# Third and fourth column groups of the modulation: steps of four contraction tiles instead of two

## The chip, the cores and the metric

The kernel runs on one core of a Trainium2 chip. The metric is the device time of one execution in microseconds (us). The time before is 2145.62 us, the median of three runs that lay between 2143.08 and 2147.35 us. A profile is one further execution with its own time.

The engines are named as in the profile: PE is the matrix engine (PEld its loading of the stationary operand), DVE the vector engine, ACT the scalar engine, POOL the general one, and SP issues almost all DMA transfers, in one queue that it works through in order.

## The reference, cut to what matters

One encoder layer on x of 1024 x 2048, all in 32-bit floats. What the change touches is the first line of it, the modulation of the normalized input by the condition c:

```python
mod = silu(c) @ w_ada + b_ada            # c: 2048, w_ada: 2048 x 6144
shift, scale, gate = split(mod, 3)
h = rmsnorm(x, pre_g) * (1 + scale) + shift
proj = h @ w_in                          # 2048 x 4608, and h @ w_merge, 2048 x 4096
...
```

The rest (windowed attention, multi-scale pooling, two gated branches, the output projection and a second norm) follows and is not touched.

## The kernel before, in words

**Products.** A big product is made in blocks of 256 output columns. Each block is one call of `strassen` and takes seven smaller products in place of eight. The banks that they sum into are called X, V and Z, so on PE one reads the sequence X, V, Z, X, V, Z and a last Z, which comes two products later, behind the first two of the next block (`run` calls `flush` there). A 32-bit operand is split into two parts (names ending in `h`/`l`, and `whi`/`wlo` for weights), and each product has the three part products high-high, low-high and high-low. ACT makes the high part (line 95), DVE the low one (line 96).

**The ramp.** At the start not all of h is there. So the first four blocks (`RAMP = 4`) are made in two halves: first over contraction groups j = 0 and 1 (`ramp_gen(0, i)`), where a product is six matmuls on PE, and later over j = 2 and 3 (`ramp_gen(1, i)`), with the first half's results loaded back and added. `fill(j)` multiplies two row tiles of x by the scale and adds the shift, and makes from them the seven split moving operands (B11, T3, T2, B21, T4, T1, B22) of group j. It needs `modc[..., j]`, which is what the change is about.

**The modulation.** `modulation(j, ...)` makes shift and scale of column group j: silu(c) times 16 contraction tiles of w_ada, each 128 x 512. The stationary operand `scz[:, kc, :]` has 32 columns, of which one is used, so a matmul takes a quarter of the array's columns; tile `kc` goes to quarter `kc % 4` and to 32 of the 128 partitions of a bank named GEMV (line 453). Each 32-bit matmul stands in the profile as two, so 16 tiles are 32 rows there. After the last tile ACT copies the bank (`acc`), PE adds up the four quarters (bank PM, line 424), and DVE adds the bias (`modc`, line 428). Groups 0 and 1 run before the ramp. The third and fourth (j = 2 and 3) are cut into eight steps of two tiles each, put into a queue `side`, 16 steps long. Three of them run before the ramp; then `run` takes one out after each step of the ramp's blocks (I call these places slots, numbered from 0). With `pin` the tile framework keeps these matmuls in the place where the code has them; other instructions are ordered by the framework's own scheduler.

**Where the tiles come from.** The 16 tiles of group j = 2 are loaded by `ada_slots(2)`, each in a buffer of its own (line 438). Those of j = 3 lie in five buffers of two tiles each, loaded ahead (`ada_tile`, line 417); buffers six to eight reuse the first three, so that their loads wait until PE has read the old tiles. In SP's queue these late loads stand behind the stores of the first ramp block's results (`ramp_d`, line 311).

Of the kernel before, what the change touches and what calls it, by code (L numbers as in the profile page):

```python
# [42 lines left out]
def encoder_layer(ctx: ExitStack, tc: tile.TileContext, x, c, table, w_ada, b_ada, pre_g,  # L43
# [32 lines left out]
    def uid(s):  # L76
        cnt[0] += 1
        return f"{s}_{cnt[0]}"

    def bank(tag, name="b"):  # L80
        return psum.tile([P, 512], F32, tag=tag, name=uid(name), bufs=1 if tag in SEEDED else 2)
# [268 lines left out]
    for r0, src in ((0, c[0]), (16, b_ada[0, 0:D]), (32, b_ada[0, D:2 * D]),  # L350
                    (48, pre_g[0]), (64, b_merge[0]), (96, pool_scale[0])):
        n = src.shape[0] // P
# [68 lines left out]
    def sum_columns(acc):  # L421
        pm = bank("at", "PM")
        for g in range(4):
            nc.tensor.matmul(pm[:, g:g + 1], acc[:, g, :], ones, start=True, stop=True)
        return pm

    def mod_columns(j, pm):
        tc.keep_in_program_order(nc.vector.tensor_tensor(
            modc[:, :, :, j], pm[:, 0:4].rearrange("p (g h) -> p g h", g=2),
            cols[:, 16:48].rearrange("p (g k) -> p g k", g=2)[:, :, 2 * j:2 * j + 2], ALU.add))  # L430
        nc.vector.scalar_tensor_tensor(modc[:, 1, :, j], modc[:, 1, :, j], 1.0,
                                       cols[:, 48 + 2 * j:50 + 2 * j], op0=ALU.add, op1=ALU.mult)

    def ada_slots(j):
        tiles = []
        for kc in range(KT):
            tiles.append(slot("ada", F32, (P, 4, P)))
            load(tiles[kc].rearrange("p (g h) n -> p g (h n)", g=2),
                 w_ada[kc * P:(kc + 1) * P, 0:2 * D].rearrange("p (g n) -> p g n", g=2)
                 [:, :, j * 256:(j + 1) * 256])  # L440
        return tiles

    def modulation(j, tile_of, pin=False):

        st_ = {}

        def step(q):
            if q == 0:
                st_["pv"] = bank("at", "GEMV")
            pv = st_["pv"]  # L450
            for kc in (2 * q, 2 * q + 1):
                g = kc % 4 * 32
                ins = nc.tensor.matmul(pv[g:g + 32, :], scz[:, kc, :], tile_of(kc), start=kc < 4,  # L453
                                       stop=kc >= 12, tile_position=(0, g))
                if pin:
                    tc.keep_in_program_order(ins)
            if q == 7:
                acc = xa2.tile([P, 4, P], F32, tag="acc", name=uid("acc"), bufs=2)
                tc.keep_in_program_order(
                    nc.scalar.activation(acc, pv.rearrange("p (g n) -> p g n", g=4), AF.Copy))  # L460
                mod_columns(j, sum_columns(acc))

        return [lambda q=q: step(q) for q in range(8)]

    def weigh(acc, t, kc):

# [7 lines left out]
    def modulation_steps(j):  # L474

        st_ = {}

        def step(q):
            if q == 0:
                st_["acc"] = xa2.tile([P, 4, P], F32, tag="acc", name=uid("acc"), bufs=2)  # L480
            if q == 8:
                mod_columns(j, st_["pm"])
                return
            acc = st_["acc"]
            at = ada_tile(j, q)
            for kk in range(2):
                kc = q * 2 + kk
                weigh(acc, at[:, kk], kc)
            if q == 7:
                st_["pm"] = sum_columns(acc)  # L490

        return [lambda q=q: step(q) for q in range(9)]
# [46 lines left out]
    ada = [ada_slots(0), ada_slots(1)]  # L539
# [8 lines left out]
            ada3.append(ada_tile(3, kc // 2))  # L548
        return ada3[kc // 2][:, kc % 2]

    side = deque(modulation(2, ada[2].__getitem__, True) + modulation(3, tile3, True))
    for s in range(2):
        for si in range(4 * s, 4 * s + 4):
            norm_rows(si)
# [16 lines left out]
        nc.tensor.matmul(bank(tag, "OPEN"), hi[:, 0:P], hi, start=True, stop=True)  # L571


    for _ in range(3):
        side.popleft()()
    parts = {}
    for i in range(RAMP):
# [126 lines left out]
    side = deque(s_ for j in range(4, 8) for s_ in modulation_steps(j))  # L704
# [47 lines left out]
    def x_step(n):  # L752
        if n < 2 * NB:
            held[n] = fetch_x(n // 2, n % 2)
        if n >= 2:
            turn_x((n - 2) // 2, n % 2, held.pop(n - 2))

    side = deque(lambda n=n: x_step(n) for n in range(2 * NB + 2))
# [17 lines left out]
    side = deque()  # L776
# [12 lines left out]
    with pool("attn") as ap:  # L789
        kv = {}  # L790

        def take_kv(kvh, what):
            hi = ap.tile([P, S], F32R, tag=what + "hi", name=uid(what))
            lo = ap.tile([P, S], F32R, tag=what + "lo", name=uid(what))
            col = (COL_K if what == "k" else COL_V) + kvh * P
            for s in range(2):
                sl = slice(s * 512, (s + 1) * 512)
                raw = ap.tile([P, 512], F32, tag="raw", name=uid("kvr"), bufs=2)
                load(raw, proj_d[col:col + P, sl])
                src = raw  # L800
                if what == "v":
                    src = bank("at")
                    for j in range(4):
                        nc.tensor.transpose(src[:, j * P:(j + 1) * P], raw[:, j * P:(j + 1) * P], ident)
                split(hi[:, sl], lo[:, sl], src)
            kv[what] = (hi, lo)


        qraw, q, bt, g, pr, pv = {}, {}, {}, {}, {}, {}
# [3 lines left out]
        def fetch_q(u):  # L813
            hp, j = UNITS[u]
            for e in range(2):
                h = 2 * hp + e
                if j == 0:
                    bt[e] = ap.tile([P, SPAN], F32, tag=f"bt{e}", name=f"bt{h}")
                    load(bt[e], bass.AP(bias_d.tensor, bias_d[h].offset + 127, [[LINE - 1, P], [1, SPAN]]))
                qraw[e] = ap.tile([P, 512], F32, tag="raw", name=uid("qr"), bufs=2)  # L820
                load(qraw[e], proj_d[COL_Q + h * P:COL_Q + (h + 1) * P, j * P:j * P + 512])

        def split_q(e):
            hi = ap.tile([P, 512], F32R, tag=f"qhi{e}", name=uid("qhi"))
            lo = ap.tile([P, 512], F32R, tag=f"qlo{e}", name=uid("qlo"))
            nc.scalar.activation(hi, qraw[e], AF.Copy, scale=P ** -0.5)
            nc.vector.scalar_tensor_tensor(lo, qraw[e], P ** -0.5, f32(hi), op0=ALU.mult, op1=ALU.subtract)
            q[e] = hi, lo
# [36 lines left out]
        def turn(u, e):  # L865
            _, n = blk(UNITS[u][1])
            if e == 0:
                pv[u] = [ap.tile([P, 3, 2, P], F32R, tag=f"pp{i}", name=uid("pp")) for i in range(2)]
            p = pr.pop((u, e))
            pt = bank("at", "PT")  # L870
            for i in range(n):
                nc.tensor.transpose(pt[:, i * P:(i + 1) * P], p[:, i * P:(i + 1) * P], ident)
            split(pv[u][0][:, 0:n, e], pv[u][1][:, 0:n, e], pt[:, 0:n * P].rearrange("p (b q) -> p b q", b=n))

        def values(u):
            hp, j = UNITS[u]
            b0, n = blk(j)
            (vhi, vlo), (phi, plo) = kv["v"], pv.pop(u)
            po = bank("at", "PV")[:, 0:2 * P]
            for i in range(n):  # L880
                ks = slice((b0 + i) * P, (b0 + i + 1) * P)
                nc.tensor.matmul(po, vhi[:, ks], phi[:, i], start=i == 0, stop=False)
                nc.tensor.matmul(po, vhi[:, ks], plo[:, i], start=False, stop=False)
                nc.tensor.matmul(po, vlo[:, ks], phi[:, i], start=False, stop=i == n - 1)
            qs = slice(j % 4 * P, (j % 4 + 1) * P)
            for e in range(2):
                nc.vector.tensor_tensor(g[e][:, qs], po[:, e * P:(e + 1) * P], g[e][:, qs], ALU.mult)
                if j % 4 == 3:
                    h = 2 * hp + e
                    store(ya_d[h * P:(h + 1) * P, (j - 3) * P:(j + 1) * P], g[e])  # L890

        def step(u, e):
            nu = len(UNITS)
            if e == 0 and 0 <= u - LAG_V < nu:
                values(u - LAG_V)
            if 0 <= u - LAG_T < nu:
                turn(u - LAG_T, e)
            if u < nu:
                if u % 16 == 0 and e == 0:
                    take_kv(UNITS[u][0] * 2 // GQA, "k")  # L900
                if u % 4 == 0:
                    split_q(e)
                scores(u, e)
            if e == 1:
                if u % 4 == 3 and u + 1 < nu:
                    fetch_q(u + 1)
                c_ = u - LAG_V + 1
                if 0 <= c_ < nu:
                    if c_ % 16 == 0:
                        take_kv(UNITS[c_][0] * 2 // GQA, "v")  # L910
                    if c_ % 4 == 0:
                        open_gate(c_)
# [372 lines left out]
    side = deque()  # L1285
# [123 lines left out]
```

## Time and profile before

| what | value |
|---|---|
| median of the runs | 2145.62 us (2143.08 to 2147.35) |
| the profiled execution, its own time | 2142.59 us |
| its span, first to last instruction | 2140.8 us |
| PE busy | 2096.1 us, 98% of the span |
| DVE busy | 1537.3 us, 72% |
| ACT busy | 1129.5 us, 53% |
| mean granted clock of PE | 0.997 |
| DMA moved | 466.11 MB, 218 GB/s in the mean |

The profiled execution lies 3.0 us below the median of the runs, and its time is 1.8 us above its span. A row of a timeline gives start, duration, engine, line, operation, what it writes and reads, shapes and a count; behind it, in brackets, the engine's idle time just before and what ended it. Matmuls overlap, and their ends are modelled, so distances are best read from start to start.

### The profile page before, as it was taken

The page shows a single profiled execution, that of the slowest core. Times are in us where ns is not written, and L with a number is a line of the kernel's source. Part 1 is how long each engine was busy: PE and PEld are TensorE (multiplying, and loading weights), DVE is VectorE, ACT ScalarE, POOL GpSimd, SP SyncE. Part 2 cuts the span into 40 slices and gives each one's busy share as a digit, 9 for nine tenths or more (in the row PEclk, how much of TensorE's full clock was granted, in tenths as well). Part 3 has the DMA queues.
Part 4 walks back from the last instruction along what each step waited for, and adds up shares of the span by engine and source line. Part 5 has one row for each costly group of instructions (what it writes and reads, how often), then busy time and mean ns, then how long its engine had stood idle before and what let it go on. Part 6 is the DMA issues. An engine that isn't in the chain of part 4 may idle for free.

```text
span 2140.8 us, 28950 instructions
## 1 busy us (share of the span) xinstructions
PE 2096.1 (98%) x9567; PEld 1715.2 (80%) x9567; DVE 1537.3 (72%) x2754; ACT 1129.5 (53%) x2124; POOL 7.4 (0%) x66
## 2 busy tenths in 40 slices
PE   6999999999999999999999999999999999999998
PEld 4588888887878888888888888888788888778886
DVE  5786666777547676777776788666956977879667
ACT  5654444443474546767775433333645644667654
POOL 0000000000000000000000000000000000000000
PEclk9999999999999999999999999999999999999999
DMA  9986566898766356445454766765655655696996
GB/s 331 292 277 202 188 207 202 305 315 270 237 216 213 122 169 207 157 156 197 150 165 154 235 214 203 242 193 171 228 170 166 213 192 164 219 298 219 303 306 240
DMA packets 303255, 466.11 MB, mean 218 GB/s; under 512 B 23882, under 2 KB 144866, under 8 KB 303104
## 3 DMA queue, kind: packets, MB, share of 16 engines
q1 hardware_dynamic: 301648, 462.02, 65.6%
q0 software_dynamic: 1120, 2.19, 0.3%
q8 instruction: 75, 1.23, 0.2%
q14 instruction: 76, 0.62, 0.1%
q10 hardware_dynamic: 336, 0.06, 0.0%
HBM read 340.41 MB, written 125.85 MB: 218 GB/s over the span
## 4 chain that ended last, share of the span: by engine, by line
PE 80%; DMA 8%; DVE 7%; issue 2%; ACT 2%; SPq 0%; ACTq 0%; DVEq 0%
PE Z L235 26%; PE V L235 18%; PE X L235 17%; PE Z L1139 2%; PE Z L1141 2%; PE Z L1140 2%; DVE wlo L96 2%; DMA raw<-in_w_merge_dram 1%; PE V L1141 1%; PE V L1139 1%; PE V L1140 1%; PE X L1141 1%; PE X L1140 1%; PE X L1139 1%; PE GEMV L453 1%
## 5 line engine op out<-in xcount | busy, mean ns | idle before, releaser
L95 ACT ACTIVATE whi<-raw 128x512 fp32r<-128x512 f32 (+1 forms) x528 | 319.7, 609 | 504.5 <-PE Z L235 252.6
L96 DVE TENSOR_TENSOR wlo<-raw,whi 128x512 fp32r<-128x512 f32 (+1 forms) x528 | 346.6, 662 | 189.8 <-PE Z L235 116.5
L96 DVE TENSOR_TENSOR wlo<-wr,whi 128x512 fp32r<-128x512 f32 x224 | 151.1, 689 | 60.9 <-ACT whi L95 58.5
L95 ACT ACTIVATE whi<-wr 128x512 fp32r<-128x512 f32 x224 | 138.5, 629 | 92.8 <-DVE wlo L96 35.9
L102 DVE TENSOR_TENSOR raw<-raw,raw 128x512 f32<-128x512 f32 x80 | 55.2, 690 | 94.2 <-DMA raw<-in_w_merge_dram 70.8
L1078 ACT ACTIVATE gt<-gt,cols 128x512 f32<-128x512 f32 x64 | 46.1, 722 | 96.2 <-DMA gt<-proj_d 77.8
L235 PE MATMUL V<-T3h,whi 128*128 128x512 f32 x336 | 92.9, 396 | 3.3 <-DVE u L102 3.3
L235 PE MATMUL X<-B11h,whi 128*128 128x512 f32 x336 | 92.4, 393 | 1.7 <-DVE part L102 0.9
L235 PE MATMUL Z<-B22h,whi 128*128 128x512 f32 x336 | 92.4, 395 | 0.8 <-ACT u L290 0.8
L235 PE MATMUL V<-T4h,whi 128*128 128x512 f32 x336 | 92.0, 393 | 0.4 <-ACT T4h L95 0.4
L235 PE MATMUL Z<-T1h,whi 128*128 128x512 f32 x336 | 91.8, 392 | 0.3 <-ACT T1h L95 0.3
L235 PE MATMUL V<-T3l,whi 128*128 128x512 f32 x336 | 91.5, 392 | 0.0
L235 PE MATMUL Z<-T1l,whi 128*128 128x512 f32 x336 | 91.1, 390 | 0.2
L235 PE MATMUL X<-B11l,whi 128*128 128x512 f32 x336 | 91.1, 390 | 0.2 <-DVE B11l L96 0.2
L235 PE MATMUL Z<-T2h,whi 128*128 128x512 f32 x336 | 91.2, 392 | 0.0
L235 PE MATMUL V<-T4l,whi 128*128 128x512 f32 x336 | 91.0, 390 | 0.0
L235 PE MATMUL X<-B21h,whi 128*128 128x512 f32 x336 | 90.9, 391 | 0.0
L235 PE MATMUL V<-T4h,wlo 128*128 128x512 f32 x336 | 90.8, 390 | 0.0
L235 PE MATMUL Z<-B22l,whi 128*128 128x512 f32 x336 | 90.8, 390 | 0.0
L235 PE MATMUL Z<-T1h,wlo 128*128 128x512 f32 x336 | 90.8, 390 | 0.0
L235 PE MATMUL Z<-T2l,whi 128*128 128x512 f32 x336 | 90.7, 390 | 0.0
L235 PE MATMUL V<-T3h,wlo 128*128 128x512 f32 x336 | 90.6, 390 | 0.0
(306 smaller groups left out, 4847.0 us busy)
## 6 DMA issues: line engine op xcount, KB each, us to landing
part<-part_d SPq DMA_DIRECT2D x136, 256.0 KB, 4.8
ada<-in_w_ada_dram SPq DMA_DIRECT2D x128, 256.0 KB, 4.7
raw<-in_w_in_dram SPq DMA_DIRECT2D x64, 512.0 KB, 4.1
raw<-in_w_merge_dram SPq DMA_DIRECT2D x64, 512.0 KB, 5.7
wr<-ws_dS SPq DMA_DIRECT2D x64, 512.0 KB, 5.3
wr<-in_w_out_dram SPq DMA_DIRECT2D x48, 512.0 KB, 5.0
proj_d<-part SPq DMA_DIRECT2D x68, 256.0 KB, 2.2
sw<-in_w_out_dram SPq DMA_DIRECT2D x64, 256.0 KB, 5.4
```

Of the source, the lines that this page charges most:

```text
L95: ins = (nc.scalar.activation(hi, src, AF.Copy), nc.vector.tensor_tensor(lo, src, f32(hi), ALU.subtract))
L96: nc.vector.tensor_tensor(lo, src, f32(hi), ALU.subtract))
L102: return (eng or nc.vector).tensor_tensor(o, a, b, ALU.add)
L235: nc.tensor.matmul(ps, w_[:, i], op[mov][j][m_], start=fresh and i == 0 and n == 0, stop=i == nj - 1 and n == 2, skip_group_check=True)
L453: ins = nc.tensor.matmul(pv[g:g + 32, :], scz[:, kc, :], tile_of(kc), start=kc < 4, stop=kc >= 12, tile_position=(0, g))
L1078: nc.scalar.activation(gt, gt, AF.Sigmoid, bias=cols[:, col:col + 1])
L1139: nc.tensor.matmul(pb, hi, w[0], start=first, stop=False, skip_group_check=True)
L1140: nc.tensor.matmul(pb, lo, w[0], start=False, stop=False, skip_group_check=True)
L1141: nc.tensor.matmul(pb, hi, w[1], start=False, stop=last, skip_group_check=True)
```

## The change

A step now sums four tiles, one for each quarter of the array's columns, and a group has four steps instead of eight. The fourth group's steps no longer follow one another from slot to slot: the queue is padded with empty steps, so that they stand at its places 6, 9, 12 and 15. Two steps instead of three run before the ramp, so in slots the third group's last steps stand at 0 and 1 (before: 0 to 4), and the fourth group's at 4, 7, 10 and 13 (before: 5 to 12).

```diff
-            for kc in (2 * q, 2 * q + 1):
+            for kc in range(4 * q, 4 * q + 4):
                 g = kc % 4 * 32
                 ins = nc.tensor.matmul(pv[g:g + 32, :], scz[:, kc, :], tile_of(kc), start=kc < 4,
                                        stop=kc >= 12, tile_position=(0, g))
                 if pin:
                     tc.keep_in_program_order(ins)
-            if q == 7:
+            if q == 3:
                 acc = xa2.tile([P, 4, P], F32, tag="acc", name=uid("acc"), bufs=2)
...
-        return [lambda q=q: step(q) for q in range(8)]
+        return [lambda q=q: step(q) for q in range(4)]
...
-    side = deque(modulation(2, ada[2].__getitem__, True) + modulation(3, tile3, True))
+    side = deque(modulation(2, ada[2].__getitem__, True))
+    for n, step in zip((6, 9, 12, 15), modulation(3, tile3, True)):
+        side.extend([lambda: None] * (n - len(side)) + [step])
...
-    for _ in range(3):
+    for _ in range(2):
         side.popleft()()
```

All that the change moves lies in the first ramp half. Behind the first product of the third ramp block, PE's instructions stand in the same order in both programs. Two places show what moved.

The first is PE at the fourth group's first step. Before, this step (tiles `ada_388`, both halves of one buffer) stands after the fifth product of the first ramp block (bank V, operand T4):

```order
L235 MATMUL V_740<-T4h_367,wlo_798 128x512
L453 MATMUL GEMV_809<-ada_388,scz 32x512 x2
L235 MATMUL Z_739<-T1h_311,whi_812 128x512
L235 MATMUL Z_739<-T1h_371,whi_812 128x512
L235 MATMUL Z_739<-T1l_312,whi_812 128x512
L235 MATMUL Z_739<-T1l_372,whi_812 128x512
L235 MATMUL Z_739<-T1h_311,wlo_813 128x512
L235 MATMUL Z_739<-T1h_371,wlo_813 128x512
L453 MATMUL GEMV_809<-ada_391,scz 32x512 x2
```

Now it stands one product earlier, after the fourth (bank X, operand B21), and takes the tiles of two buffers:

```order
L235 MATMUL X_740<-B21h_363,wlo_784 128x512
L453 MATMUL GEMV_797<-ada_388,scz 32x512 x2
L453 MATMUL GEMV_797<-ada_391,scz 32x512 x2
L235 MATMUL V_742<-T4h_307,whi_802 128x512
L235 MATMUL V_742<-T4h_367,whi_802 128x512
L235 MATMUL V_742<-T4l_308,whi_802 128x512
```

So tile 3 of the group (second half of `ada_391`) is wanted two products earlier than before, and three full products now follow without a step between.

The second place is PE at the third step of the fourth group. Before, tiles 8 and 9 (`ada_400`) and 10 and 11 (`ada_889`, the sixth buffer) had a product between them:

```order
L453 MATMUL GEMV_809<-ada_400,scz 32x512 x2
L235 MATMUL Z_829<-T2h_299,whi_877 128x512
L235 MATMUL Z_829<-T2h_359,whi_877 128x512
L235 MATMUL Z_829<-T2l_300,whi_877 128x512
L235 MATMUL Z_829<-T2l_360,whi_877 128x512
L235 MATMUL Z_829<-T2h_299,wlo_878 128x512
L235 MATMUL Z_829<-T2h_359,wlo_878 128x512
L453 MATMUL GEMV_809<-ada_889,scz 32x512 x2
```

Now the four stand together after that product:

```order
L235 MATMUL Z_829<-T2h_359,wlo_876 128x512
L453 MATMUL GEMV_797<-ada_400,scz 32x512 x2
L453 MATMUL GEMV_797<-ada_889,scz 32x512 x2
L235 MATMUL X_828<-B21h_303,whi_894 128x512
```

The loads of the sixth to eighth buffers keep their places in SP's queue: behind the stores of the first ramp block, and the eighth buffer's second half behind that block's last store.

## The prediction

> **What bounds the kernel now.** I read the page's head first, then busy time by stretch, then PE's timeline through the ramp, then SP's queue and its landings.
>
> ```profile
> span 2140.8 us, 28950 instructions
> PE 2096.1 (98%) x9567; PEld 1715.2 (80%) x9567; DVE 1537.3 (72%) x2754; ACT 1129.5 (53%) x2124; POOL 7.4 (0%) x66
> ```
> ```profile
> 60.00:78.00 18.00, 17.10 (x73) 8.19 (x74) 14.15 (x30) 11.69 (x23) 0.00 (x0) 1.00 1.08 348
> 78.00:96.00 18.00, 18.00 (x77) 9.38 (x76) 11.68 (x25) 10.15 (x21) 0.00 (x0) 1.00 0.74 233
> 96.00:114.00 18.00, 18.00 (x81) 14.90 (x80) 17.23 (x38) 15.28 (x34) 0.00 (x0) 1.00 0.85 268
> ```
> (Columns: stretch, length, busy time of PE, PEld, DVE, ACT, POOL, granted clock, DMA share, GB/s.) PE sets the time nearly everywhere, so PE time taken out of a stretch without PE idling shortens the run. But up to 78 us the DMA engines are full (348 GB/s), and what PE does there waits for tiles. After 78 us DMA has room, while weight loads of PE (9.38 of 18) show that PE's time goes elsewhere: into the steps.
>
> PE's timeline:
>
> ```profile
> 57.52 2.42 PE L453 MATMUL GEMV<-ada,scz 128*32 128x512 f32 x12
> ...
> 65.63 1.07 PE L453 MATMUL GEMV<-ada,scz 128*32 128x512 f32 x8
> 66.63 0.73 PE L235 MATMUL Z<-T2l,whi 128*128 128x512 f32 x2
> 67.20 0.62 PE L235 MATMUL Z<-T2h,wlo 128*128 128x512 f32 x2
> 67.75 1.05 PE L453 MATMUL GEMV<-ada,scz 128*32 128x512 f32 x4
> 68.73 0.73 PE L235 MATMUL X<-B21h,whi 128*128 128x512 f32 x2
> ...
> 73.78 1.05 PE L453 MATMUL GEMV<-ada,scz 128*32 128x512 f32 x4
> ...
> 74.76 0.74 PE L235 MATMUL Z<-T1h,whi 128*128 128x512 f32 x2
> ...
> 77.35 0.73 PE L235 MATMUL X<-B11h,whi 128*128 128x512 f32 x2
> ...
> 79.92 0.74 PE L235 MATMUL V<-T3h,whi 128*128 128x512 f32 x2
> ...
> 82.51 0.73 PE L235 MATMUL Z<-B22h,whi 128*128 128x512 f32 x2
> ...
> 92.83 0.73 PE L235 MATMUL Z<-T1h,whi 128*128 128x512 f32 x2
> ...
> 93.86 0.95 PE L424 MATMUL PM<-ones,acc 128*128 128x1 f32 x8
> ...
> 95.21 0.63 PE L235 MATMUL X<-B11h,whi 128*128 128x512 f32 x2
> ...
> 96.60 0.62 PE L235 MATMUL V<-T3h,whi 128*128 128x512 f32 x2
> ...
> 104.77 0.62 PE L235 MATMUL X<-B11h,whi 128*128 128x512 f32 x2
> ...
> 106.13 0.62 PE L235 MATMUL V<-T3h,whi 128*128 128x512 f32 x2
> ```
>
> Three prices follow. A product without a step: 106.13 - 104.77 = 1.36 us. A product with a step of two tiles: 79.92 - 77.35 = 2.57, so the step costs 1.21. And a step of four tiles is in this trace already: at 65.63 the scheduler had put two steps together (x8). From its start to the next product are 66.63 - 65.63 = 1.00 us; the step of two at 67.75 took 68.73 - 67.75 = 0.98. Four quarters cost 0.02 more than two, so a step of four costs 1.23.
>
> SP's queue, and landings of what it issued from 65.5 us on:
>
> ```profile
> 40.17 21.12 SPq L438 DMA_DIRECT2D ada<-in_w_ada_dram  x28
> 61.35 3.86 SPq L187 DMA_DIRECT2D raw<-in_w_in_dram  x6
> 65.59 7.14 SPq L417 DMA_DIRECT2D ada<-in_w_ada_dram  x10
> ...
> 77.85 0.32 SPq L311 DMA_DIRECT2D ramp_d<-p  x1
> 78.27 2.48 SPq L417 DMA_DIRECT2D ada<-in_w_ada_dram  x5
> 85.19 0.34 SPq L311 DMA_DIRECT2D ramp_d<-c  x1
> 85.58 0.43 SPq L417 DMA_DIRECT2D ada<-in_w_ada_dram  x1
> ```
> ```profile
> ada<-in_w_ada_dram SPq DMA_DIRECT2D x10, 256.0 KB, 6.0
> ```
> ```profile
> DMA to landing us min/median/max: 2.7/3.5/6.4
> ```
> (The last row is line 417's, all 80 loads.) The third group's last tile is the last of the 28 (21.12 us, 0.75 each), so it is issued at about 60.4 and lands at about 66.4; ten tiles of the fourth group follow from 65.59 at 0.75 us each, so its tiles 0 to 3 land at 71.6, 72.3, 73.1 and 73.8 and tile 7 at 76.8.
>
> **The change, part by part.** *Visits.* Before, PE leaves the products 12 times for a step in the ramp (13 slots, two of them run together at 65.63); now 6 times. That would be six visits, 6 x 1.21 = 7.3 us, if PE were never held up.
>
> *The third group, slots 0 and 1, and tiles 6 and 7 before the ramp.* Moving these tiles forward costs nothing and gains little: what covers it is the landing. PE waits for tile 7 (about 60.4), for tile 11 (63.4) and for tile 15 (66.4), each time with one product ready in between. Tile 15 plus 1.0 lets the third product start at 67.4; with its 1.36, the PM matmuls (1.0, below) and the fourth product's 1.36 plus 0.3 of switching PE comes to the fourth group's first step at about 71.4.
>
> *Its first step, slot 4.* This is a new wait: tile 3 lands at 73.8, so PE stands some 2.4 us, where before tiles 0 and 1 had long landed at the step's place (73.78). Behind it in PE's queue stands everything; ACT and DVE have earlier results to work on. The wait fixes the start of the fifth product at 73.8 + 1.0 = 74.9, however early PE comes. Products five and six and the next block's first take 1.36 each: the latter starts at 77.6, where before it started at 77.35 with the same work done. So all that the change saves up to here, it gives back: -0.2 us.
>
> *Slots 7, 10 and 13.* From here before had six visits (tiles 4 to 15), now three: 6 x 1.21 - 3 x 1.23 = 3.6 us. Step by step: V 80.2, Z 81.5, Z 82.9, step, X 85.5, V 86.8, Z 88.2, step, X 90.8. The PM matmuls, which stood in the sixth product before (95.21 - 92.83 - 1.36 = 1.0), stand in X now, so V starts at 90.8 + 1.36 + 1.0 = 93.2 against 96.60: 3.4 us. Both ways of counting give 3.3 to 3.4; I take **3.3**.
>
> *The late loads.* Tiles 10 and 11 (sixth buffer) go out behind the store of p, which came 3.1 us after its product's start (74.76 to 77.85). That product now starts at 76.2, so the loads go at 79.7 and 80.2 and land, by the 2.7 to 6.4 above, between 82.4 and 86.6; PE wants them at 84.5. Wait between 0 and 2.1; the DMA share is 0.74 there, so I take the short end, 0. Tile 15's load goes behind the store of c, whose product moves from 82.51 to 81.5: it is issued at 84.6 instead of 85.58 and with a median landing of 3.5 is there at 88.1; wanted at 89.8: 0.
>
> *DVE.* It was busy 17.23 of 18 us from 96 to 114 with `fill(3)` and the weight splits. `modc` of the fourth group comes only 1.8 us earlier (its PM needs ACT's copy of the bank and starts at about 92.0 instead of 93.86), PE 3.3 us, so DVE could give back up to 1.5 us. The order now puts more weight splits ahead of `fill(3)`, and what that fill makes is wanted a whole block later (114 us): I take 0, and keep 1.5 for the range.
>
> *After the ramp* order is unchanged, and PE idles little:
>
> ```profile
> PE b L745 <- ACT xt L739: 4.1, 2, 2.6
> PE V L235 <- DVE u L102: 3.3, 2, 2.5
> ```
> ```profile
> 503.35 2.08 PE L235 MATMUL V<-T3h,whi 128*128 128x512 f32 x4 [2.46 <-DVE u L102]
> 505.23 1.72 PE L235 MATMUL V<-T3l,whi 128*128 128x512 f32 x4
> 506.78 1.09 PE L235 MATMUL V<-T3h,wlo 128*128 128x512 f32 x4
> ```
> ```profile
> 46.00:54.00 8.00, 8.00 (x33) 2.06 (x34) 6.84 (x13) 4.75 (x8) 1.22 (x11) 1.00 1.10 349
> 500.00:510.00 10.00, 7.54 (x27) 5.75 (x27) 9.25 (x13) 2.66 (x5) 0.00 (x0) 0.83 0.73 248
> ...
> 600.00:650.00 50.00, 45.86 (x228) 37.54 (x226) 22.84 (x35) 36.38 (x95) 0.00 (x0) 1.00 0.72 236
> ```
>
> These waits hang on loads that PE's progress lets go, so they move with it. Sum: 2142.6 - 3.3 = 2139.3 us for the profiled execution's like, which lies 3.0 under the median; for the median 2145.6 - 3.3 = **2142.3**.
>
> **The clock.** Behind the wait at 503.35 eight matmuls took 3.43 us (to 506.78) instead of 8 x 0.227 = 1.8 at the product's usual rate (1.36 / 6), and the granted clock of that stretch is 0.83: half for 3.4 us, a price of 1.6 us. From 46 to 54 us, where PE did almost nothing but steps at the pace of landings, it stayed 1.00. So I expect no half clock from the new wait at 71.4. The wait of 2.6 us for ACT xt, in the stretch from 600 to 650, left the clock at 1.00 too: of two waits of like length one halved it. [...]
>
> **The rivals.** (1) *All six visits are saved.* For: PE is 98% busy. Against: the landing at 73.8. 2145.6 - 7.3 = 2138.3. (2) *The half clock at 503 falls away* (or that wait shrinks), for as the waits of 2.5 and 2.6 us show, length alone doesn't bring it: 2145.6 - 3.3 - 1.6 = 2140.7. Against: nothing in the change touches that wait. (3) *The new wait halves the clock* in the ramp: 2145.6 - 3.3 + 1.6 = 2143.9; against it stands the row of 46 to 54. (4) *The gain is given back later*, DVE's 1.5 first and the rest in the waits for ACT xt and DVE u, if their loads go out at their own pace rather than PE's: 2145.6. (5) *Slower:* tile 15's load, alone behind the store of c, comes late. ACT's copies cost 0.61 us each:
>
> ```profile
> L95 ACT ACTIVATE whi<-raw 128x512 fp32r<-128x512 f32 (+1 forms) x528 | 319.7, 609 | 504.5 <-PE Z L235 252.6
> ```
>
> Should ACT make eight copies of `fill(2)` ahead of c (4.9) and the queue be as full as at 65 us (6.0), the tile lands 10.9 us after 88.1, at 99.0; PE then waits 9.2, and the time is 2145.6 - 3.3 + 9.2 = 2151.5. It decides when tile 15 lands after 97.4 (89.8 + 3.3 + 4.3). Against: c went out 2.7 us after its product's start before.
>
> **How the numbers follow.** 0.2% is 4.3 us, about what a measurement of this kernel can tell from no change. Forecast 0.42, (1) 0.18, (2) 0.24, (3) 0.04, (4) 0.05, (5) 0.07. The forecast, (3) and (4) lie within 0.2%: 0.51; (1) and (2) are faster: 0.42; slower 0.07. The range goes from (1) with the runs' scatter, 2137.3, to (4) with some, 2146.5; it leaves out (5) and tails. The forecast alone has 2140.5 to 2144.2 (tiles 10 and 11 up to 2.1 late).
>
> **What would show it.** GEMV matmuls in rows of x8; a step of four of about 1.0 us to the next product; PE waiting for ada some 2.4 us before the fourth group's first step, and the fifth product at 74.9; the third block's first V at about 93.2 instead of 96.6, with everything behind it 3.3 us earlier. If PE reaches 77.6 later, or a wait stands before the step at 84.5, terms are wrong; if the first V is at 93 and the end isn't earlier, (4) holds.

## The result, and the profile after

| | before | after |
|---|---|---|
| median of the runs, us | 2146.41 (2142.49 to 2152.86) | 2142.23 (2137.56 to 2147.82) |
| ratio, with its 95% interval | | 0.9982 (0.9974 to 0.9989) |
| the profiled execution, us | 2142.59 | 2137.56 |

The change makes the kernel 0.18% faster, 1.1 to 2.6 thousandths. That is 3.9 us, between 2.4 and 5.6. The forecast was 3.3 less, 2142.3. The kernel before ran 0.8 us slower beside it than in the runs shown ahead, so it is the gain that is to be compared, more than the time.

The page's head of the changed kernel:

```profile
span 2135.8 us, 28949 instructions
PE 2091.6 (98%) x9567; PEld 1714.1 (80%) x9567; DVE 1536.7 (72%) x2754; ACT 1129.4 (53%) x2124; POOL 7.4 (0%) x66
```

As many matmuls as before, 4.5 us less of PE's busy time. Not all of that is the change: 1.6 us of it is a stretch at half clock near 503 us that this profile lacks (its granted clock from 500 to 510 us is 1.00, against 0.83 before), and a second profile of the changed kernel has 2095.7 us, only 0.4 less than before. Busy time by stretch, with the columns as ahead:

```profile
60.00:78.00 18.00, 17.57 (x71) 8.56 (x70) 13.58 (x29) 11.37 (x23) 0.00 (x0) 1.00 1.06 340
78.00:96.00 18.00, 18.00 (x93) 12.20 (x92) 14.72 (x32) 13.04 (x27) 0.00 (x0) 1.00 0.85 277
96.00:114.00 18.00, 18.00 (x81) 14.90 (x80) 16.33 (x37) 14.74 (x33) 0.00 (x0) 1.00 0.91 307
```

The first stretch does nearly as much as before (71 matmuls against 73), the second more (93 against 77, at 12.20 us of weight loads against 9.38), and the third the same. So the whole gain arises between 78 and 96 us. PE's timeline there (start, duration, engine, line, operation; the idle time before it in brackets):

```profile
57.46 3.93 PE L453 MATMUL GEMV<-ada,scz 128*32 128x512 f32 x16
...
67.48 0.74 PE L235 MATMUL Z<-T2h,whi 128*128 128x512 f32 x2
...
71.85 3.21 PE L453 MATMUL GEMV<-ada,scz 128*32 128x512 f32 x8 [0.42 <-DMA ada<-in_w_ada_dram]
75.00 0.74 PE L235 MATMUL V<-T4h,whi 128*128 128x512 f32 x2
...
76.50 0.63 PE L235 MATMUL Z<-T1h,whi 128*128 128x512 f32 x2
...
77.89 0.61 PE L235 MATMUL X<-B11h,whi 128*128 128x512 f32 x2
...
84.65 1.06 PE L453 MATMUL GEMV<-ada,scz 128*32 128x512 f32 x8
85.64 0.73 PE L235 MATMUL X<-B21h,whi 128*128 128x512 f32 x2
...
93.35 0.63 PE L235 MATMUL V<-T3h,whi 128*128 128x512 f32 x2
...
101.55 0.61 PE L235 MATMUL X<-B11h,whi 128*128 128x512 f32 x2
...
111.07 0.61 PE L235 MATMUL X<-B11h,whi 128*128 128x512 f32 x2
```

The second block's first product (77.89) starts 0.5 us later than before. The third block's first V starts 3.25 us earlier (93.35 against 96.60), and the fourth block's first product 3.22 us earlier (101.55 against 104.77). Matched matmul by matmul, PE stays 3.22 us ahead to 495 us. Behind that the two traces differ in the lengths of single waits, and the last matmuls are 5.1 us ahead.

For the experiments I measure in the ramp alone: from the stage's first step (the GEMV row at 57.46) to the fourth block's first product (101.55). That is 44.09 us in the changed kernel and 104.77 - 57.52 = 47.25 before. I call it the ramp's length. It counts from PE's own start, while the loads keep their own time, so a kernel whose stage starts early against its loads reads a little longer (the two profiles of the fourth group alone, below, show it).

### The profile page after: what moved, and what is told of

It reads as the page before. It is cut to its first block, busy times and chain, and to the rows that moved or that the text cites. A ratio compares the mean times of both kernels' runs of the same rounds, so it can differ in the third digit from the quotient of the medians.

```text
span 2135.8 us, 28949 instructions
## 1 busy us (share of the span) xinstructions
PE 2091.6 (98%) x9567; PEld 1714.1 (80%) x9567; DVE 1536.7 (72%) x2754; ACT 1129.4 (53%) x2124; POOL 7.4 (0%) x66
## 3 DMA queue, kind: packets, MB, share of 16 engines
q8 instruction: 75, 1.23, 0.2%
## 4 chain that ended last, share of the span: by engine, by line
PE 86%; DMA 6%; DVE 5%; issue 1%; ACT 1%; SPq 0%; ACTq 0%; DVEq 0%
PE Z L235 29%; PE V L235 19%; PE X L235 19%; DMA raw<-in_w_merge_dram 2%; PE Z L1141 2%; PE Z L1142 2%; PE Z L1143 2%; PE V L1143 1%; PE V L1141 1%; PE V L1142 1%; DVE wlo L96 1%; PE X L1143 1%; PE X L1142 1%; PE X L1141 1%; PE GEMV L453 1%
## 5 line engine op out<-in xcount | busy, mean ns | idle before, releaser
L235 PE MATMUL Z<-T2h,wlo 128*128 128x512 f32 x336 | 90.8, 390 | 0.0
L235 PE MATMUL X<-B11h,wlo 128*128 128x512 f32 x336 | 90.7, 390 | 0.0
```

The lines of the kernel that those rows point to most:

```text
L235: nc.tensor.matmul(ps, w_[:, i], op[mov][j][m_], start=fresh and i == 0 and n == 0, stop=i == nj - 1 and n == 2, skip_group_check=True)
```

## The experiments

Two theories were set against each other. *Landings* (that of the prediction): a step less is worth 1.2 us only where its tiles have landed; up to the fourth group's first step PE runs at the pace of the DMA. *Count*: each visit less is worth the same wherever it stands. A third, *given back*, says that later waits take what the ramp gains. The first four kernels below were also run once each, beside one run of the kernel before at 2147.2 us: third group alone 2143.12, fourth group alone 2138.78, two slots later 2142.52, one quarter 2156.52. Runs of one kernel scatter by some 10 us, so the ramp's length decides there.

### The third group alone

```diff
-    for n, step in zip((6, 9, 12, 15), modulation(3, tile3, True)):
+    for n, step in zip(range(7, 15), modulation(3, tile3, True, 2)):
```

(`modulation` takes the number of tiles per step as its last argument.)

> The third group in steps of four, as in the change; the fourth in steps of two, in the old places (slots 5 to 12). Read on PE's timeline: start of the fourth ramp block's first product (104.77 us before, 101.55 after). Landing theory (a step costs PE 1.2 us only where its tiles are there; before the fourth group's first step PE runs at the pace of the landings): the fifth product starts at about 71.3, the step with tiles 0 and 1 comes at 72.6, the next at 75.0 with tile 3 landed at 73.8, so 1.3 us are won ahead of the second block and all is kept: 103.5. Count of visits (each step less is worth 1.21 us wherever it is): two steps less than before in the ramp's slots, 102.4. If the third group's part is worth nothing at all: 104.8.

PE's timeline:

```profile
57.14 3.94 PE L453 MATMUL GEMV<-ada,scz 128*32 128x512 f32 x16
...
103.17 0.62 PE L235 MATMUL X<-B11h,whi 128*128 128x512 f32 x2
```

The ramp's length is 46.03 us, 1.2 less than before; 1.3 was expected by the landings, 2.4 by the count. This kernel's stage began 0.4 us early, so the position itself (103.17) reads lower than the 103.5 expected; the length is the better measure. The third group's move is worth a little by itself. In the change even that is lost, since the fourth group's first step waits.

### The fourth group alone

```diff
-    side = deque(modulation(2, ada[2].__getitem__, True))
-    for n, step in zip((6, 9, 12, 15), modulation(3, tile3, True)):
+    side = deque(modulation(2, ada[2].__getitem__, True, 2))
+    for n, step in zip((8, 11, 14, 17), modulation(3, tile3, True)):
...
-    for _ in range(2):
+    for _ in range(3):
```

> The third group in steps of two, as before; the fourth in steps of four at slots 5, 8, 11 and 14, so that its first step stands where before the first step of two stood, at 73.8. Landing theory: tile 3 lands as PE arrives, the sixth product starts at 74.8 as before, and from there four steps less one price each: 7 x 1.21 - 3 x 1.23 = 4.8 us less, the fourth block's first product at 100.0, earlier than in the change (101.55), though it makes fewer changes. Count of visits: the change with six visits less got 3.2, this one with four less gets 2.1: 102.6.

> The fourth group alone in steps of four, at slots 5, 8, 11 and 14, timed. If what is won in the ramp reaches the end, the median is 4.75 us below the kernel before, 0.9978, 1.5 us below the change. If later waits take a part of it back, it is no better than the change: 0.9982 to 0.999.

PE's timeline in the first profile, and then in the second:

```profile
58.22 2.41 PE L453 MATMUL GEMV<-ada,scz 128*32 128x512 f32 x12
...
74.47 1.16 PE L453 MATMUL GEMV<-ada,scz 128*32 128x512 f32 x8
...
100.72 0.62 PE L235 MATMUL X<-B11h,whi 128*128 128x512 f32 x2
```
```profile
57.17 2.41 PE L453 MATMUL GEMV<-ada,scz 128*32 128x512 f32 x12
...
73.47 1.88 PE L453 MATMUL GEMV<-ada,scz 128*32 128x512 f32 x8
...
100.43 0.62 PE L235 MATMUL X<-B11h,whi 128*128 128x512 f32 x2
```

The lengths are 42.50 and 43.26 us: 4.75 and 4.0 less than before, where the landings gave 4.8 and the count 2.1. A kernel that removes fewer visits gains more in the ramp than the change. The two profiles also show how near the edge this place is. In the first, tile 3 lands at 74.54 with PE there at 74.47. In the second it lands at 74.26, but PE is there at 73.47 (its stage began 1.05 us earlier, the landing came only 0.28 earlier), and the row of the step is 1.88 us long instead of 1.16. The time is 0.9985 of the kernel before (0.9975 to 0.9994), 1.3 to 5.4 us less. That holds 4.0 to 4.75, but it doesn't show this kernel ahead of the change.

### The change, with the fourth group two slots later

```diff
-    for n, step in zip((6, 9, 12, 15), modulation(3, tile3, True)):
+    for n, step in zip((8, 11, 14, 17), modulation(3, tile3, True)):
```

> The change, with the fourth group's four steps two slots later (6, 9, 12, 15): its first step comes when tile 3 has landed. Landing theory: fifth product at 71.3, sixth at 72.6, step at 74.0 without a wait, second block's first product at 75.0 (77.89 in the change); from there three steps in each: the fourth block's first product at 98.7, 2.9 us earlier than in the change, and the run about 2139.4. Rival, the gain is limited by what follows the step (DVE's fill for the second half, or late loads): the steps end 0.6 us later than in the change, and a wait of up to 2.9 us shows before the second half's first product (111.07 in the change) or before the steps at 84 and 90; then no gain over the change.

> The change with the fourth group's steps two slots later, timed. If what is won in the ramp reaches the end: 6.1 us below the kernel before, 0.9972, and 2.9 us below the change. Its first profile had the 6.1 us in the ramp, but ended only 0.3 us of span ahead: if that was the kernel and not chance (loads that go at their own pace, or waits that begin wherever PE comes early), the ratio is 0.998 to 1.000 and the profile shows the loss between 900 and 1350 us again.

PE's timeline in the first profile:

```profile
57.97 3.90 PE L453 MATMUL GEMV<-ada,scz 128*32 128x512 f32 x16
...
74.34 1.07 PE L453 MATMUL GEMV<-ada,scz 128*32 128x512 f32 x8
75.34 0.73 PE L235 MATMUL X<-B11h,whi 128*128 128x512 f32 x2
...
99.14 0.62 PE L235 MATMUL X<-B11h,whi 128*128 128x512 f32 x2
```

And in the second:

```profile
58.54 3.90 PE L453 MATMUL GEMV<-ada,scz 128*32 128x512 f32 x16
...
99.67 0.62 PE L235 MATMUL X<-B11h,whi 128*128 128x512 f32 x2
```

The first step takes 1.00 us to the next product, without a wait (tile 3 landed at 74.28). The ramp's length is 41.17 us, and 41.13 in the second profile: 6.1 less than before and 2.7 to 2.9 less than in the change's two profiles, as expected by the landings. So the 2.4 us that PE stood for tile 3 are to be had, and with them most of the 6 x 1.21 that the prediction counted, by two more empty places in the queue. In the ramp, DVE's `fill(3)` and the late loads take nothing of it.

The first profile's span is only 0.1 us shorter than that of the kernel before (2140.7), and the second's 0.7 longer. By the runs the kernel is at 0.9968 (0.9954 to 0.9982), 3.9 to 9.9 us less. So the gain as a whole is not given back, though single profiles seemed to say so; whether a part of up to 2 us is lost, the interval leaves open.

### All of a step's tiles in one quarter of the array

```diff
-                g = kc % 4 * 32
+                g = (q if pin else kc % 4) * 32
```

(with `start` and `stop` set for each quarter's first and last tile)

> The change, but all four tiles of a step go to the same quarter of the array's columns, one quarter per step, instead of to one quarter each. The same number of visits, matmuls and loads. Read: from the start of the fourth group's second and third step to the next product (1.00 and 0.99 us in the change). If a step of four costs as little as one of two because the four quarters work at the same time: four tiles one after another, about 0.9 us each as the quarters' 0.98 for a step of one tile per quarter suggests, 3.6 to 3.9 us per step. If the price is the switching of the array and the matmuls themselves run at the products' 0.227 us: 8 x 0.227 = 1.8 us. If only the visit counts: 1.0 us. The two late steps then cost 5.6, 1.6 or 0 us, and the fourth block's first product moves by that or more against 101.55.

PE's timeline at the fourth group's second step:

```profile
85.10 3.62 PE L453 MATMUL GEMV<-ada,scz 128*32 128x512 f32 x8
88.65 0.73 PE L235 MATMUL V<-T3h,whi 128*128 128x512 f32 x2
...
114.96 0.62 PE L235 MATMUL X<-B11h,whi 128*128 128x512 f32 x2
```

3.55 us from the step to the next product, against 1.00 with one tile in each quarter. The two later steps take 3.55 as well. A tile takes 3.55 / 4 = 0.89 us (an estimate that spreads over the four tiles whatever the visit itself costs; the steps of eight below give 1.85 - 1.00 = 0.85 for one more tile in each quarter). So the four quarters run at the same time almost entirely. That is why four tiles cost what two did: the old step left two quarters empty. Of a step's price of 1.2 us, 0.85 to 0.89 is the time of one tile, and 0.3 to 0.4 are left (an estimate, from these numbers); no run shows what they are spent on. The ramp's length is 56.71, and the one run took 2156.52 us beside 2147.2 for the kernel before.

### Two steps of eight

If a visit costs some 0.3 us beside its tiles, fewer and longer visits should gain a little more.

```diff
-    for n, step in zip((6, 9, 12, 15), modulation(3, tile3, True)):
+    for n, step in zip((10, 17), modulation(3, tile3, True, 8)):
         side.extend([lambda: None] * (n - len(side)) + [step])
+    side[11] = lambda: [tile3(kc) for kc in (10, 12, 14)]
```

> The third group as in the change; the fourth in two steps of eight tiles, at slots 8 and 15, with the three late loads issued from the code right behind the first of them. In the kernel with one quarter per step a tile behind another in the same quarter cost 0.89 us (3.55 for four). So a step of eight, two tiles in each quarter, takes 1.0 + 0.89 = 1.9 us to the next product and costs about 2.1; two of them 4.2 against 4.9 for four steps of four. First step at about 76.8, as tile 7 lands; the fourth block's first product 0.7 us earlier than with the steps at slots 6, 9, 12 and 15, that is 6.8 us earlier than before. If the late loads come late (they go 2.7 us later than there): a wait before the second step, at about 90 us, of up to 4 us. If the gain reaches the end: 0.9968.

PE's timeline:

```profile
57.97 3.91 PE L453 MATMUL GEMV<-ada,scz 128*32 128x512 f32 x16
...
77.08 1.92 PE L453 MATMUL GEMV<-ada,scz 128*32 128x512 f32 x16
...
98.41 0.62 PE L235 MATMUL X<-B11h,whi 128*128 128x512 f32 x2
```

The next product starts at 78.93, so a step of eight takes 1.85 us, and so does the second (88.72 to 90.57), without a wait for the late loads. The ramp's length is 40.44, 6.8 less than before, as expected. The time is 0.9967 of the kernel before (0.9955 to 0.9979), as with steps of four at the later slots. Another 0.7 us is below what these runs can tell.

### The third group's last eight tiles in one step too

```diff
-    side = deque(modulation(2, ada[2].__getitem__, True))
+    third = modulation(2, ada[2].__getitem__, True)
+    side = deque(third[:2] + [lambda: None] * 3 + [lambda: (third[2](), third[3]())])
```

(on top of the kernel with two steps of eight)

> As the kernel with two steps of eight, but the third group's tiles 8 to 15 also in one step of eight, behind the third product, when all have landed; before, PE waited for tiles 11 and 15 in two steps of 1.6 us each in that place. If those waits for landings are what holds PE there, one step of 2.1 us takes the place of 3.2 and of a price of about 0.2: 1.3 us less, fourth block's first product 39.1 us behind the stage's first step (40.44 there). If DVE's low part of T3, which comes at 65.0 in that kernel and is wanted by the second product, is late next: the second product ends at 65.5 at the earliest, the third at 66.9, the step at 68.8, with 1.0 for PM still to come, against 70.2 there: 0.4 less, 40.0. Timed: 0.9960 by the first, 0.9966 by the second.

PE's timeline:

```profile
58.13 3.92 PE L453 MATMUL GEMV<-ada,scz 128*32 128x512 f32 x16
...
64.19 0.47 PE L235 MATMUL V<-T3h,whi 128*128 128x512 f32 x1 [0.78 <-ACT T3h L95]
...
67.15 2.06 PE L453 MATMUL GEMV<-ada,scz 128*32 128x512 f32 x16
...
98.91 0.61 PE L235 MATMUL X<-B11h,whi 128*128 128x512 f32 x2
```

The length is 40.77, 0.3 more than with the third group's tiles in two steps: neither 1.3 nor 0.4 less, so both theories missed. PE now stands 0.78 us for ACT's high part of T3, which the steps covered before and which neither theory had in its sum (the second spoke of DVE's low part). The loads also came later in this profile. The third group's last tile landed at 68.12 us instead of 66.76, and the step that needs it took 1.99 us (67.15 to 69.14) where a step of eight without a wait takes 1.85. The fourth group's loads went out from 67.40 instead of 66.03, its tile 7 landed at 78.44 where PE was there at 77.39, and its first step took 2.07 us. These two waits, 0.14 and 0.22 us, are about the 0.3 us; the fifth product starts 13.70 us behind the stage's first step (71.83 - 58.13), against 13.57 (71.54 - 57.97) with two steps. Whether the edit made the loads late or chance did, the runs don't show. So moving these steps gained nothing here, and whether PE would be held by the tiles or by T3 stays open. By the runs, 0.9972 (0.9959 to 0.9984), the kernel is not told apart from the two kernels with later slots and with steps of eight.

### The two kernels again

> The changed kernel once more, to stand beside the next three on the same chip, and for a second profile of it. Both theories of the start: third block's first V some 3.2 us earlier than before. If the differences behind the ramp (waits at 500 to 640, 1330 to 1400, from 1815 on) are chance, this profile has others than the first; if they belong to the kernel, they come again. Against the kernel before: 0.9985, as the 3.2 us give, or 0.998 as measured at first.

> The kernel before once more, for a second profile. If the waits behind the ramp (503, 616, 640, 1012, 1331, 1398 us in the first) are chance in their lengths, they differ here by some tenths to 2 us each, and the sum of the differences from 130 us to the end is of the size of the differences between the changed kernel's two profiles, 5 us. The distance from the first step of the stage (57.52 in the first) to the fourth block's first product (104.77) is 47.25 again within 0.2.

The changed kernel's second set of runs gives 0.9982 again (0.9971 to 0.9993). Its second profile:

```profile
57.79 3.88 PE L453 MATMUL GEMV<-ada,scz 128*32 128x512 f32 x16
...
101.62 0.62 PE L235 MATMUL X<-B11h,whi 128*128 128x512 f32 x2
```

The ramp's length is 43.83 us (101.62 - 57.79), 3.4 less than before. The kernel before, in its second profile:

```profile
58.38 2.38 PE L453 MATMUL GEMV<-ada,scz 128*32 128x512 f32 x12
...
105.63 0.62 PE L235 MATMUL X<-B11h,whi 128*128 128x512 f32 x2
```

47.25 again. But its span is 2149.3 us against 2140.8: 0.8 of the 8.5 us lies ahead of 500 us, the rest in the waits behind it, where some 5 were expected. The changed kernel's second profile (span 2141.4) has no gain left at its end against the first profile of before, and neither the wait of 2.79 us at 520.67 that the first had nor its undisturbed clock near 503 (0.83 from 500 to 510 us, against 1.00 in the first). Four matmuls behind the wait there took 1.72 us:

```profile
502.28 1.72 PE L235 MATMUL V<-T3h,whi 128*128 128x512 f32 x4 [3.03 <-DVE u L102]
```

So the 1.9 us that the first two profiles differ in beyond the ramp (5.1 against 3.2) are no more than this scatter, and single ends of profiles of this kernel tell nothing below some 9 us.

| kernel | ramp's length, us | less than 47.25 | ratio to before (95%) |
|---|---|---|---|
| third group alone | 46.03 | 1.2 | - |
| the change | 44.09, 43.83 | 3.2, 3.4 | 0.9982 (0.9974 to 0.9989) |
| fourth group alone | 42.50, 43.26 | 4.75, 4.0 | 0.9985 (0.9975 to 0.9994) |
| the change, two slots later | 41.17, 41.13 | 6.1 | 0.9968 (0.9954 to 0.9982) |
| two steps of eight | 40.44 | 6.8 | 0.9967 (0.9955 to 0.9979) |
| third group in one step too | 40.77 | 6.5 | 0.9972 (0.9959 to 0.9984) |

The ramp explains each ratio within its interval. By the runs all kernels with a ratio are faster than the kernel before. Against the change the intervals of the fourth and fifth row still overlap its own; on the chip where they ran side by side, their medians were 2143.31 and 2142.31 us against 2145.01 for the change. The 2.7 to 2.9 us that the later slots are ahead of it in the ramp stand in both profiles.

## Why the prediction was right, point by point

- **The time.** Forecast 3.3 us less, measured 3.9 (2.4 to 5.6). That the median itself, 2142.23, lies within 0.1 us of the forecast 2142.3 is luck, since the runs scatter by 10 us and the kernel before ran 0.8 us slower beside it. What bears the forecast out is the ramp: 3.2 and 3.4 us less in two profiles, step by step as follows.
- **Prices.** Right. A product still takes 1.36 us ((111.07 - 101.55) / 7). A step of four takes 0.99 from its start to the next product (84.65 to 85.64), as read from the row at 65.63 before (1.00). That row was the whole basis for "four cost what two did". The one-quarter kernel shows why it holds (3.55 us with the four tiles in one quarter). The 0.3 us of switching that the prediction counts ahead of the fourth group's first step is shown by no run: a product ahead of a step takes 1.45 (83.20 to 84.65), 0.09 more than 1.36.
- **The third group.** Right: the third product starts at 67.48 (67.4 forecast), at the pace of the landings. Alone the move is worth 1.2 us.
- **The new wait at the fourth group's first step.** Right, and the step on which everything hung. PE was there at 71.43 (71.4 forecast; the row at 71.85, less its 0.42 idle), tile 3 landed at 73.98 (73.8), V T4 started at 75.00 (74.9). The trace puts only 0.42 us down as idle, the wait for tile 0: tiles 1 to 3 then landed some 0.75 us apart, and PE ran each as it came (matmuls started at 71.85, 72.52, 73.28 and 74.02), which counts as busy. The row's 3.21 us show the wait, against 1.06 without one. The kernel with the steps two slots later, which lacks it, gains 2.7 to 2.9 more.
- **Up to the second block's first product.** Forecast -0.2 us, measured -0.5 (77.89 against 77.35): the products behind the step took 1.50 and 1.39 (75.00, 76.50, 77.89) rather than 1.36 each. A part of a step's price lies in the product behind it: 1.21 to 1.23 in all, but only 1.00 from its start to that product.
- **Slots 7, 10 and 13.** Forecast 3.6, measured 3.8 (from X to the third block's first V 15.46 us instead of 19.25). The two small errors are opposite, which is luck: 3.25 in sum, where 3.3 was taken.
- **Late loads and DVE, both taken at 0.** Right. The five loads went out at 79.85, where 79.7 was forecast, and tile 15's at 84.84 (84.6):

```profile
79.85 2.46 SPq L417 DMA_DIRECT2D ada<-in_w_ada_dram  x5
...
84.84 0.43 SPq L417 DMA_DIRECT2D ada<-in_w_ada_dram  x1
```

 No step waits for them, and the second half's first product starts 3.22 us earlier too (111.07 against 114.29), so nothing is given back to `fill(3)`.
- **Rivals.** *All six visits saved* (2138.3) is refuted for this change by tile 3; with the later slots 6.1 of its 7.3 us are there in the ramp. *The half clock at 503 falls away*: it did in the first profile (granted clock 1.00 from 500 to 510 us), but in the second it stood there again (0.83), with some also from 600 to 650 (0.97), and the kernel before had none from 500 to 510 in its second profile (1.00). So it is no effect of the change, and the chance of 0.24 was too high. *The new wait halves the clock*: the granted clock is 1.00 from 60 to 114 us. *Given back*: not as a whole, by the ratios of the kernels with 6.1 and 6.8 us; some 2 us of loss they leave open. *Tile 15 late*: no wait.
- **What was not seen.** The prediction took the slots as given and did not work out that two empty places more would nearly have doubled the gain in the ramp, though it had all the numbers for it: a landing at 73.8 and PE there at 71.4.

## What to carry to other kernels

Where a step waits for a load, saving instructions ahead of it was worth nothing here (with three visits fewer ahead of it, the second block's first product came 0.5 us later): compare the time at which PE arrives with the landing, and place the step behind it. A matmul that fills a part of the array's columns cost the same here whether the other quarters worked or not (0.98 us for two quarters, 1.00 for four), so fill them before counting visits. With an effect of a few us in a run that scatters by 10, measure a stretch with fixed ends in each profile, and leave the total to many runs.

## What the runs showed of the clock

The prediction could not say why one wait of 2.5 us halved PE's clock and one of 2.6 did not. The runs don't show why; they show that the length of a wait alone doesn't decide it. In the first profile of before, as the wait of 2.46 us at 503.35 ended (columns as above: length, busy time of PE and the rest, then the granted clock):

```profile
503.16:506.57 3.41, 3.22 (x8) 2.55 (x9) 3.41 (x5) 0.00 (x0) 0.00 (x0) 0.50 0.84 256
```

The clock is 0.50 for 3.41 us. Behind the prediction's wait of 2.6 us, which ended at 640.42 in the same profile, it stays at 1.00:

```profile
639.69:643.10 3.41, 2.68 (x14) 2.30 (x15) 1.39 (x2) 3.17 (x9) 0.00 (x0) 1.00 0.87 272
```

In the kernel with the third group alone it stays at 1.00 after a wait of 3.40 us. First the row of the timeline, then the stretches:

```profile
503.36 1.20 PE L235 MATMUL V<-T3h,whi 128*128 128x512 f32 x4 [3.40 <-DVE u L102]
```
```profile
501.65:505.06 3.41, 1.70 (x7) 1.42 (x8) 3.38 (x6) 0.00 (x0) 0.00 (x0) 1.00 0.75 270
505.06:508.47 3.41, 3.41 (x16) 2.82 (x15) 3.41 (x5) 1.43 (x3) 0.00 (x0) 1.00 0.80 221
```

And in the first profile of the fourth group alone a wait of 2.42 us was followed by half clock:

```profile
1326.23 1.20 PE L235 MATMUL X<-B11h,whi 128*128 128x512 f32 x4 [2.42 <-DVE part L102]
```
```profile
1327.76:1331.17 3.41, 3.41 (x10) 2.64 (x9) 3.41 (x20) 2.00 (x3) 0.00 (x0) 0.50 0.49 158
```

So in these profiles half clock came with waits of 2.42 and 2.46 us and not with waits of 2.6 and 3.40. With it, the wait at 503 cost 1.6 us more than its length (an estimate: 3.43 us for the eight matmuls behind 503.35, less 8 x 0.227). What decides whether it comes is not shown.
